# First norm of a hybrid layer: four of sixteen token tiles transposed by TensorE instead of by DMA

## The chip, the cores and the metric

The kernel runs on one core of a Trainium2 chip. The metric is the device time of one execution in microseconds. Engines are named as in the profile: PE is TensorE, DVE VectorE, ACT ScalarE, POOL GpSimd; SP is SyncE, which issues most DMAs.

## The reference

One layer, on x of 2048 tokens by 1024 columns in float32:

```
h = RMSNorm(x, g_mix);  z = h @ w_in          # columns: conv u | gate B | gate C | q | k | v
yA = B * causal_dwconv3(C * u)
yB = three dilated sliding-window attentions over 8 heads, mixed by their softmax sums
x = x + concat(RMSNorm(yA), RMSNorm(yB)) @ w_out
x = x + SwiGLU(RMSNorm(x))                    # 2816 hidden columns
```

The change sits in the first line: the norm of x, and the transposed form of h that the matmuls of w_in need.

## The kernel before, in words

Every large product is done in float16 with each factor split in a high part and a remainder ("hi" and "lo"); `mm3_steps` issues three matmuls for each 128 rows of the contraction (L187 to L189: high x high, high x low, low x high).

**The first norm.** The 2048 tokens are 16 tiles of 128 (`norm`, L248). For each tile the 128x1024 float32 block is loaded by SP (`nx_x`, for tiles 6 and 7 `qT`; L257), ACT squares it and sums the squares (L258), a short chain on ACT and DVE makes the reciprocal root (`rnorm`, L65 to L70), ACT writes the high part (L262) and DVE the remainder (L263) into a float16 tile `ka` or `kb`. Two DMA transposes, one for the high part and one for the remainder, then write them into `self.x[c][q]` (`b` in the profile), with the model's columns on the partitions; c is the chunk of 512 tokens, q is 0 for high and 1 for remainder. The profile shows these DMAs at L195. There are two buffers each of `ka` and `kb`, which the convolution also uses, so a later batch of tiles waits until the transposes of an earlier one have been read out.

**The matmuls around it.** `in_and_conv` first does tiles 0 to 3 (two calls of `norm`) with the weights of the first column group between them: `first(2)`, `first(0)`, `first(1)` load 128 columns each (`wraw`, L131), find their largest value on DVE (`vmax`, L92 on) and write them as high part (ACT, L145) and remainder (DVE, L146) into `wq`. Then `conv_steps` goes through four chunks c of 512 tokens. In each it does three groups of 24 matmuls (C, u and B, in this order) into PSUM tiles `cvx`, `cvx` and `mm`. The very first group is done in two halves of 256 tokens, so that it needs tiles 0 and 1 alone at first. Ahead of chunk c the function `before(c)` asks for the norm of the four tiles of chunk c+1. This is column group j=0; for j=1 and j=2 the chunks are gone through again with weights that are loaded and split meanwhile. The loads for j=1 are ordered behind the last transposes of the norm:

```python
with tc.issue_after(self.dve.ins), tc.issue_after(self.sp.ins):
    u1 = self.weights(cols(j + 1), ux, dst=(t1[:, 0], t1[:, 1]))[2]
```

Attention, the output projection and the SwiGLU follow; PE is busy nearly throughout.

**What sets the order.** Each engine works through its own queue in order. The order in the queues isn't written out: the framework's planner lays it out from the dependences and its own estimate of times (`schedule_with_timeline_sim=True`), earlier lines of the program going first where several are ready. `issue_after` adds single edges. SP's queue is in order too: a load behind a transpose waits until it has been issued.

PSUM has 8 banks here: 3 of `psmm` (tile `mm`), 4 of `cvx`, 1 of `pstr`.

Of the kernel before, what the change touches and what calls it, by code (L numbers as in the profile page):

```python
# [8 lines left out]
F32 = mybir.dt.float32  # L9
F16 = mybir.dt.float16  # L10
# [7 lines left out]
P = 128  # L18
S = 2048
D = 1024  # L20
KC = D // P
# [8 lines left out]
class Builder:  # L30
# [203 lines left out]
    def setup(self):  # L234

        nc, A, cp = self.nc, self.A, self.cp
        self.g_in = self.gains(cp, [A["g_mix"][0]], "gin", 0)
        make_identity(nc, self.ident32)
        nc.vector.memset(self.ones, 1.0)
        for i, b in enumerate(self.SHIFTS):  # L240
            nc.vector.memset(self.eps[:, i:i + 1], 4.0 ** -b * EPS)
        nc.scalar.square(self.ones, self.ones)
        self.yamax = cp.tile([P, 16], F32, name="yamax")
        self.ssa = cp.tile([P, NT], F32, name="ssa")
        self.uq = cp.tile([P, 5], F32, name="uq")
        self.uo = cp.tile([P, 2], F32, name="uo")
        self.wc = cp.tile([P, 4, 3], F32, name="convw")
        for t in range(3):  # L248
            nc.scalar.dma_start(self.wc[:, :, t], A["conv_w"][0, t].rearrange("(c p) -> p c", p=P))

    def norm(self, i, xt, hl):

        nc = self.nc
        n = len(xt)
        ss = self.nxs.tile([P, n], F32, name=f"nx_ss{n}")
        for j in range(n):
            nc.sync.dma_start(xt[j], self.A["x"][0][(i + j) * P:(i + j + 1) * P])  # L257
            nc.scalar.activation(hl[j][:, 0], xt[j], AF.Square, accum_out=ss[:, j:j + 1])  # L258
        r = self.rnorm(self.nxs, ss, n, D, f"nx{n}", 9)
        for j in range(n):  # L260
            h, l = hl[j][:, 0], hl[j][:, 1]
            nc.scalar.activation(h, xt[j], AF.Copy, scale=r[:, j:j + 1])  # L262
            self.dve = nc.vector.scalar_tensor_tensor(l, xt[j], r[:, j:j + 1], h, op0=ALU.mult, op1=ALU.subtract)  # L263
            c, t = (i + j) // 4, slice((i + j) % 4 * P, ((i + j) % 4 + 1) * P)
            for q in range(2):
                self.sp = self.transpose(self.x[c][q][:, :, t], hl[j][:, q])

# [95 lines left out]
    def in_and_conv(self):  # L363
        tc, nc, A = self.tc, self.nc, self.A
        w_in, w_out = A["w_in"][0], A["w_out"][0]
        with ExitStack() as c:
# [36 lines left out]
            for j in range(3):  # L403
                def before(c):
                    if j == 0 and c == 0:
                        norm(0, 2)
                        first(2)
                        norm(2, 2)
                        first(0)
                        with tc.issue_after(self.dve.ins):  # L410
                            first(1)
                    if j == 0 and c < 3:
                        if c == 2:
                            norm(4 * c + 4, 2)
                            norm(4 * c + 6, 2)
                        else:
                            norm(4 * c + 4, 4)
# [786 lines left out]
```

## Time and profile before

| | us |
|---|---|
| median of 3 runs | 2199.42 (2199.12 to 2206.35) |
| the profiled execution | 2203.85 |
| its span, first to last instruction | 2202.1 |
| PE busy in it | 2075.1 (94%) |
| DVE busy | 1458.2 (66%) |
| ACT busy | 1028.2 (47%) |
| POOL busy | 627.1 (28%) |

Times in the profile are microseconds from the start of the span. PE's busy time counts pipelined matmuls, so a busy PE is not one at its peak. A row of a timeline gives start, duration, engine, line, operation, out<-in with shapes, and how many were merged; brackets give the idle time before it and what ended it. SPq is the DMA queue of SP, and the duration of an issue there is the time that SP spent on it, not the time to landing.

### The profile page before, as it was taken

The page shows a single profiled execution, that of the slowest core. Times are in us where ns is not written, and L with a number is a line of the kernel's source. Part 1 is how long each engine was busy: PE and PEld are TensorE (multiplying, and loading weights), DVE is VectorE, ACT ScalarE, POOL GpSimd, SP SyncE. Part 2 cuts the span into 40 slices and gives each one's busy share as a digit, 9 for nine tenths or more (in the row PEclk, how much of TensorE's full clock was granted, in tenths as well). Part 3 has the DMA queues.
Part 4 walks back from the last instruction along what each step waited for, and adds up shares of the span by engine and source line. Part 5 has one row for each costly group of instructions (what it writes and reads, how often), then busy time and mean ns, then how long its engine had stood idle before and what let it go on. Part 6 is the DMA issues. An engine that isn't in the chain of part 4 may idle for free. (4 is left out here: it accounts for less than half of the span.)

```text
span 2202.1 us, 32820 instructions
## 1 busy us (share of the span) xinstructions
PE 2075.1 (94%) x11864; PEld 1080.4 (49%) x11864; DVE 1458.2 (66%) x3380; ACT 1028.2 (47%) x2134; POOL 627.1 (28%) x515
## 2 busy tenths in 40 slices
PE   4999999989889889979999999999999989999999
PEld 2344567767666644434444444444444434444444
DVE  5687447778876676785767676766676565545454
ACT  6443347676766655653333343333333243434341
POOL 0000133344343212212112111211121145555463
PEclk9999999999999989989999999999999999999999
DMA  9767458999989987899332233223322754251342
GB/s 244 168 201 245 110 121 150 197 180 184 178 163 211 213 206 220 246 280 244 101 105 87 96 110 100 92 87 110 101 91 91 242 195 140 59 191 53 116 142 96
DMA packets 555492, 339.64 MB, mean 154 GB/s; under 512 B 354624, under 2 KB 508224, under 8 KB 552896
## 3 DMA queue, kind: packets, MB, share of 16 engines
q1 hardware_dynamic: 537648, 314.38, 55.4%
q10 hardware_dynamic: 17680, 23.16, 3.0%
q8 instruction: 93, 1.52, 0.3%
q14 instruction: 71, 0.58, 0.1%
HBM read 161.24 MB, written 107.54 MB: 122 GB/s over the span
## 5 line engine op out<-in xcount | busy, mean ns | idle before, releaser
L1001 PEld LDWEIGHTS <-w 128*128 128x128 f16 x3696 | 362.6, 98 | 457.3 <-issue 18.4
L1001 PE MATMUL ps<-b,w 128*128 128x512 f16 x2112 | 465.4, 381 | 10.9 <-ACT s L1050 3.5
L1126 PE MATMUL ps<-b,w 128*128 128x512 f16 x1848 | 402.3, 381 | 6.2 <-ACT s L1137 5.3
L1001 PE MATMUL ps<-hb,w 128*128 128x512 f16 x1584 | 348.9, 380 | 4.9 <-DVE w_m L77 2.6
L1126 PEld LDWEIGHTS <-w 128*128 128x128 f16 x1848 | 181.4, 98 | 226.8 <-issue 10.6
L894 POOL TENSOR_TENSOR t<-wq 128x512 f32<-128x512 f32 (+1 forms) x46 | 60.4, 1312 | 442.5 <-issue 266.9
L187 PE MATMUL mm<-wq,b 128*128 128x384 f16 x512 | 170.9, 334 | 7.4 <-DVE vs L471 7.4
L1007 DVE TENSOR_TENSOR s<-ps,s 128x512 f32<-128x512 f32 x220 | 150.2, 683 | 36.4 <-PE ps L1001 35.8
L188 PE MATMUL mm<-wq,b 128*128 128x384 f16 x512 | 170.5, 333 | 0.0
L189 PE MATMUL mm<-wq,b 128*128 128x384 f16 x512 | 170.2, 332 | 0.0
L1133 POOL TENSOR_TENSOR x<-x,s 128x512 f32<-128x512 f32 x72 | 103.5, 1438 | 188.6 <-DVE s L1144 140.7
L1134 DVE SCALAR_TENSOR_TENSOR x<-ps,a_u,x 128x512 f32<-128x512 f32 x96 | 71.9, 750 | 109.3 <-PE ps L1126 80.7
L615 ACT ACTIVATE s<-s,u 128x256 f32<-128x256 f32 (+1 forms) x224 | 98.0, 452 | 66.5 <-DVE u L610 44.9
L911 ACT CAST w<-t 128x512 f16<-128x512 f32 x88 | 54.1, 617 | 142.0 <-PE ps L1001 75.6
L187 PEld LDWEIGHTS <-b 128*128 128x128 f16 x768 | 84.4, 110 | 70.7 <-ACT b L773 8.2
L610 DVE CUSTOM_DVE_ANT_0 s<-s,mask,nkap 128x256 f32<-128x256 f32 (+1 forms) x224 | 104.5, 482 | 20.0 <-PE s L605 14.4
L188 PEld LDWEIGHTS <-b 128*128 128x128 f16 x768 | 84.6, 110 | 65.2 <-issue 16.7
L189 PEld LDWEIGHTS <-b 128*128 128x128 f16 x768 | 84.2, 110 | 57.2 <-issue 5.4
L187 PE MATMUL cvx<-b,wq 128*128 128x512 f16 (+1 forms) x200 | 77.4, 390 | 31.3 <-ACT kb L262 25.0
L633 PE MATMUL av<-v,et 128*128 128x65 f16 x1800 | 78.5, 196 | 28.6 <-DMA et<-eh 19.0
L604 PE MATMUL s<-ka,qT 128*128 128x128 f16 (+1 forms) x408 | 91.1, 270 | 7.6 <-DVE eh L626 6.6
L1113 ACT CAST w<-t 128x512 f16<-128x512 f32 (+1 forms) x96 | 53.6, 581 | 90.6 <-PE ps L1126 75.3
(297 smaller groups left out, 3802.6 us busy)
## 6 DMA issues: line engine op xcount, KB each, us to landing
d_a<-a ACTq DMA_DIRECT2D x88, 256.0 KB, 2.0
d_wd<-w SPq DMA_DIRECT2D x77, 256.0 KB, 2.0
wq<-d_a SPq DMA_DIRECT2D x64, 256.0 KB, 4.1
b<-d_wd SPq DMA_DIRECT2D x14, 1024.0 KB, 7.7
wraw<-in_w_in_dram SPq DMA_DIRECT2D x24, 512.0 KB, 7.3
d_h<-hl SPq DMA_DIRECT2D x24, 512.0 KB, 3.0
wq<-in_w_gate_dram SPq DMA_DIRECT2D x22, 512.0 KB, 5.3
wq<-in_w_up_dram SPq DMA_DIRECT2D x22, 512.0 KB, 5.3
```

The costliest lines, as they stand in the source:

```text
L187: self.pe = mm(ps, lhsT=lh(k), rhs=rh(k), start=k == ks[0], stop=False)
L188: mm(ps, lhsT=lh(k), rhs=rl(k), start=False, stop=False)
L189: mm(ps, lhsT=ll(k), rhs=rh(k), start=False, stop=k == ks[-1])
L604: nc.tensor.matmul(o, lhsT=query(u), rhs=hi[x], start=True, stop=False)
L610: nc.vector.tensor_tensor_reduce(sm[:, at[u]], sp[:, at[u]], mask[:, P - P * has_prev(u):256], accum_out=Ub[:, u, HD + 1:HD + 2], op0=ALU.add,
L615: nc.scalar.activation(sm[:, at[u]], sm[:, at[u]], AF.Exp, scale=-1.0, bias=Ub[:, u, HD + 1:HD + 2])
L633: self.pe_av = nc.tensor.matmul(av[:, u - u0], lhsT=p_, rhs=v_, start=n_ == 0, stop=n_ == len(ops) - 1)
L1001: nc.tensor.matmul(ps[self.BANK[n]], lhsT=w[:, x, k], rhs=b[:, y, k], start=first and k == 0 and q == 0, stop=k == 3 and q == 2, skip_grou ...
L1007: nc.vector.tensor_tensor(t, x, y, op=ALU.add)
L1126: nc.tensor.matmul(ps[self.BANK[n]], lhsT=L[n][:, x, f], rhs=B[n][:, f, y], start=first and f == 0 and q == 0, stop=f == n_f - 1 and q == ...
L1133: nc.gpsimd.tensor_tensor(o, o, s_, op=ALU.add)
L1134: nc.vector.scalar_tensor_tensor(o, bank, u, o, op0=ALU.mult, op1=ALU.add)
```

## The change

A float16 copy of the identity is made at setup. In `norm`, the tiles of chunk 0 (0 to 3) are no longer transposed by DMA. For each of the high part and the remainder, eight matmuls take a 128x128 block as the stationary operand and the identity as the moving one, four into one bank of `psmm`; the bank is then copied as float16 into `self.x`, by ACT for the high part and by DVE for the remainder. Tiles 4 to 15 are transposed by DMA as before. That makes 64 matmuls, 8 copies on ACT and 8 on DVE in place of 8 DMA transposes.

```diff
--- before.py
+++ after.py
@@ setup
         nc.scalar.square(self.ones, self.ones)
+        self.ident16 = cp.tile([P, P], F16, name="ident16")
+        nc.vector.tensor_copy(self.ident16, self.ident32)
@@ norm
             c, t = (i + j) // 4, slice((i + j) % 4 * P, ((i + j) % 4 + 1) * P)
+            if c < 1:
+
+                for q in range(2):
+                    for k in range(0, KC, 4):
+                        ps = self.psmm.tile([P, 4, P], F32, name="mm")
+                        for m in range(4):
+                            self.pe = nc.tensor.matmul(ps[:, m], lhsT=hl[j][:, q, (k + m) * P:(k + m + 1) * P],
+                                                       rhs=self.ident16, start=True, stop=True)
+                        (nc.vector.tensor_copy if q else nc.scalar.copy)(self.x[c][q][:, k:k + 4, t], ps)
+                continue
             for q in range(2):
                 self.sp = self.transpose(self.x[c][q][:, :, t], hl[j][:, q])
```

## Rows read from the trace of the kernel before

**Rows 1.** Busy time by stretches: stretch, length, each engine, PEclk, DMA share, GB/s.

```profile
0.00:27.00 27.00, 0.37 (x1) 0.10 (x1) 16.38 (x66) 19.68 (x37) 0.70 (x6) 1.00 1.04 255
...
260.00:2202.00 1942.00, 1855.99 (x10839) 974.45 (x10837) 1280.58 (x2968) 914.93 (x1920) 612.39 (x482) 0.98 0.57 148
```

**Rows 2.** Waits of PE: who waited for whom: total, times, longest us.

```profile
PE cvx L187 <- ACT kb L262: 25.0, 1, 25.0
...
PE cvx L187 <- ACT wq L145: 3.8, 1, 3.8
```

**Rows 3.** Timeline of PE, 27 to 104 us.

```profile
27.45 0.40 PE L188 MATMUL cvx<-b,wq 128*128 128x256 f16 x1 [2.06 <-DMA b<-ka]
27.64 0.42 PE L189 MATMUL cvx<-b,wq 128*128 128x256 f16 x1
27.85 0.42 PE L187 MATMUL cvx<-b,wq 128*128 128x256 f16 x1
...
35.85 0.40 PE L188 MATMUL cvx<-b,wq 128*128 128x256 f16 x1 [1.54 <-DMA b<-kb]
...
51.06 0.59 PE L187 MATMUL cvx<-b,wq 128*128 128x512 f16 x2
...
103.47 0.61 PE L187 MATMUL cvx<-b,wq 128*128 128x512 f16 x1 [3.76 <-ACT wq L145]
```

**Rows 4.** Timeline of SP, the DMA queue, 15 to 90 us.

```profile
15.18 10.38 SPq L195 DMA_TRANSPOSE b<-ka  x4
...
26.76 7.20 SPq L195 DMA_TRANSPOSE b<-kb  x4
34.02 1.05 SPq L257 DMA_DIRECT2D nx_x<-in_x_dram  x2
35.17 7.26 SPq L195 DMA_TRANSPOSE b<-ka  x4
42.52 6.14 SPq L195 DMA_TRANSPOSE b<-kb  x4
...
55.55 5.38 SPq L195 DMA_TRANSPOSE b<-ka  x4
...
77.23 5.43 SPq L195 DMA_TRANSPOSE b<-kb  x4
82.71 7.79 SPq L131 DMA_DIRECT2D wraw<-in_w_in_dram  x6
```

**Rows 5.** Groups by line and form: out<-in xcount, busy us, mean ns, idle.

```profile
L1007 DVE TENSOR_TENSOR s<-ps,s 128x512 f32<-128x512 f32 x220 | 150.2, 683 | 36.4 <-PE ps L1001 35.8
...
L621 ACT CAST et<-pt 128x512 f16<-128x512 f32 x40 | 24.1, 602 | 6.1 <-PE pt L620 5.8
```

**Rows 6.** Timeline of DVE, 5 to 40 us.

```profile
5.65 0.16 DVE L92 TENSOR_REDUCE vm_a<-gin_g 128x1 f32<-128x8 f32 x1 [4.70 <-DMA gin_g<-in_g_mix_dram]
...
15.12 1.22 DVE L92 TENSOR_REDUCE vm_a<-wraw 128x1 f32<-128x1024 f32 x1 [0.68 <-DMA wraw<-in_w_in_dram]
...
24.00 2.48 DVE L263 SCALAR_TENSOR_TENSOR kb<-nx_x,nx_y,kb 128x1024 f16<-128x1024 f32 x2 [1.85 <-ACT kb L262]
...
32.11 2.48 DVE L263 SCALAR_TENSOR_TENSOR ka<-nx_x,nx_y,ka 128x1024 f16<-128x1024 f32 x2
...
36.90 2.18 DVE L146 SCALAR_TENSOR_TENSOR wq<-wraw,w_sg,wq 128x128 f16<-128x128 f32 x8
```

**Rows 7.** Timeline of ACT, 21 to 33 us.

```profile
21.77 1.06 ACT L258 ACTIVATE kb<-qT 128x1024 f16<-128x1024 f32 x1 [0.85 <-DMA qT<-in_x_dram]
...
30.93 2.19 ACT L262 ACTIVATE ka<-nx_x,nx_y 128x1024 f16<-128x1024 f32 x2 [2.36 <-DVE nx_y L70]
```

**Rows 8.** Busy time by stretches of 2 us, as in rows 1.

```profile
36.00:38.00 2.00, 2.00 (x11) 1.40 (x10) 2.00 (x6) 1.53 (x6) 0.00 (x0) 0.50 0.91 295
...
44.00:46.00 2.00, 2.00 (x11) 0.92 (x10) 0.00 (x0) 1.36 (x3) 0.00 (x0) 1.00 1.07 199
52.00:54.00 2.00, 2.00 (x11) 0.91 (x10) 1.24 (x6) 1.54 (x4) 0.00 (x0) 1.00 0.95 380
```

## The prediction

> **What bounds the kernel now.** I read the busy time by stretches first. From 260 us to the end TensorE (PE) is busy for 1856 of 1942 us; in the first 27 us it does next to nothing (0.37 us) [rows 1]. So the bulk is matmul time that this edit does not touch, and what it can change is how early the first stage lets PE run on. Next I read what PE waits for: 25.0 us before its first matmul is the longest wait of the whole execution, and the other long one in the front is 3.8 us for weights [rows 2].
>
> The timeline of PE places them. After a lone first matmul the stream proper begins at 27.45, released by the DMA transposes of token tiles 0 and 1. It stops again until those of tiles 2 and 3 have landed, at 35.85. From there it runs to 51.06, where chunk c=1 begins without a stall, and the 3.8 us of weights end at 103.47 [rows 3].
>
> The timeline of the DMA queue shows the other chain. SP issues the transposes of tiles 0 to 3 from 15.18 to 25.56 and from 26.76 to 33.96, four each; those of tiles 4 to 7 follow from 35.17 to 48.66 [rows 4]. PE reaches c=1 some 2.4 us behind the last of those issues. **So c=1 starts where two chains meet, with no slack in either**: PE's work on c=0, and the SP queue's transposes for c=1. An edit that shortens one alone gives nothing. From c=1 on the second chain goes on: each batch of tiles is written into buffers that the transposes before it must have left, and the raw weights of the next column group are loaded right behind the last transposes (77.23 to 82.66, load at 82.71) [rows 4].
>
> **The change, part by part.**
>
> *Removed:* 8 DMA transposes, 10.38 + 7.20 = 17.58 us of SP's queue [rows 4]. Uncontended ones go at 5.38 us for four (from 55.55), 1.35 us each [rows 4]; these were slower because x loads shared the engines.
>
> *Added:* 64 matmuls of 128 columns, 16 copies out of PSUM (8 on ScalarE, ACT, and 8 on VectorE, DVE), and one conversion of the identity. PE spaced its 256-column matmuls by 0.21 us there (27.64 to 27.85, [rows 3]), so 128 columns are at most that and, by width, 0.107: 64 x 0.107 = 6.8 us (13.6 at the upper end). Nearly all of it falls in time in which PE stands idle and costs nothing; the eight matmuls of the last half tile, 0.9 us, lie on the path. An ACT copy of just this form (128x512, float32 in PSUM to float16) takes 602 ns [rows 5]; 8 make 4.8 us. DVE has no such row. Its two-input 128x512 sum out of PSUM takes 683 ns [rows 5], which bounds a one-input copy from above; below stands ACT's 602, and 0.6 to 0.7 us it is. I take 0.65, the middle of two near ends; 8 make 5.2 us. The identity costs nothing: DVE stands idle for 4.70 us before its first reduction at 5.65 [rows 6].
>
> *What the copies delay.* On DVE two idle times of note lie between the first normalized tiles and tiles 4 to 7, 0.68 and 1.85 us [rows 6], together 2.5; the rest is work. So 5.2 us of copies push the float16 remainders of tiles 4 to 7 (32.11 to 36.9, [rows 6]) by 5.2 - 2.5 = 2.7 us. ACT has 2.36 us of idleness just before the same tiles [rows 7] and follows DVE there; I charge it nothing of its own. The ends are 0 (the copies fit into the holes) and 5.2 (no hole is used).
>
> *PE's chain.* The remainder of tile 3 ends at 26.48 today (24.00 + 2.48, [rows 6]), and the half chunk that needs it gets under way only at 35.85 [rows 3]: 9.4 us for issue, queue and landing. In the changed kernel the copies of tiles 0 and 1 push that remainder by at most 2.6 us, less the holes: 27.6. Behind it come 0.9 us of matmuls, two copies of 0.65 and their handovers, so the half chunk starts near 30.5 instead of 35.85. The first matmuls of c=0 can start as early as 20 instead of 27.45. Chunk c=0 ends 5.3 us earlier, 45.8 instead of 51.06. The weights of its third group, written by DVE from 36.90 to 39.1 [rows 6], shift to 42 and are needed at 40.7: its first matmuls may be held for an instant. The second half of c=0's first group ran at a granted clock of 0.50, the lower level [rows 8]; were it at full clock, PE would save 2.5 us more, and only wait longer for c=1.
>
> *SP's chain, which ends last.* Today the transposes for c=1 begin at 35.17, behind those of tiles 2 and 3 and two x loads [rows 4], although tile 4 was written by ACT from 30.93 on, at 1.09 us a tile [rows 7]. With the queue free they start when tile 4 is there: 32.0 + 2.7 = 34.7. Nothing else is in the engines by then (the loads of tiles 8 to 11 have gone before), so eight go in 8 x 1.35 = 10.8 us: the last issue ends at 45.5 instead of 48.66, 3.2 us earlier. The last remainder, 36.9 + 2.7 = 39.6, does not hold that. PE arrives at 45.8 and waits until about 47.9. I round the gain to 3.0 us. Every later batch waits for transposes before it, and the 3.8 us wait for weights hangs behind the last of these; so all of it shifts by the same 3 us, and beyond 260 us PE is full.
>
> [...] From 44 to 46 us, with transposes alone in the engines, 199 GB/s moved; from 52 to 54, with x loads alone, 380 [rows 8]. [...] The measurement says half the speed, so I stay with 1.35 us each.
>
> *The sum.* Profiled execution: 2203.85 us, span 2202.06. 2203.85 - 3.0 = 2200.85. The median of the runs shown is 2199.42, 4.4 below that execution; on its scale 2199.42 - 3.0 = **2196.4 us**.
>
> **The rivals.**
> *A, the forecast:* 3 us less, 2196.4, between 2193 and 2199. Chance 0.38.
> *B, the whole lead of PE passes through:* 7.5 us (27.45 - 20) at most by c=0's start, if tiles 4 to 7 are prepared earlier as well, since with an empty queue their x arrives sooner (ACT waits for it for 0.85 us at 21.77, [rows 7]). For it: the DMA engines are full through the first 27 us (share 1.04, [rows 1]). Against: ACT and DVE, not the loads, are what precedes tiles 4 to 7. Time 2199.42 - 7.5 = 2191.9; if the 3.8 us wait for weights closes too, 2188.1. Chance 0.22.
> *C, the copies are the new bound (slower):* all 16 land ahead of tiles 4 to 7 on DVE and ACT without using a hole, and the loads of tiles 10 and 11 still share the engines with the transposes, which then take today's 7.26 + 6.14 [rows 4]. Start 32.0 + 5.2 = 37.2, end 50.6 instead of 48.66: 1.9 us late, and 5.2 if the delay meets every later batch again: 2201.3 to 2204.6. It decides from a start later than 37.8 with fast transposes, or 35.2 with slow ones. Chance 0.18. [...] No row of the kernel before shows these copies in this stage.
> *D, swallowed later:* c=1 comes early, but the weights of the next group do not, because what precedes them (the load at 82.71, then DVE and ACT) does not move; the 3.76 us wait at 103.47 grows by the gain. Against it: that load follows the last transposes in SP's order. 2199.4, chance 0.12.
> *E, a new order elsewhere:* the planner lays out all engines' queues by its own simulated times, and the edit shifts these. Later stages may come out in another order, either way by 10 us or more. Nothing in the profile measures it. Chance 0.10.
>
> **How the numbers follow.** A, D, C and most of B lie between 2187 and 2204; outside remain B's far corner (0.05), part of C (0.03) and most of E (0.09). 0.5% of this time is 11 us, about what a measurement here can tell from no change (the three runs span 7 us). Faster than 2188.4: 0.06 from B's corner and 0.06 from E, 0.12. Slower than 2210.4: 0.04 from E, 0.03 from C if its delay returns with each batch, 0.07. The rest, 0.81, is no change by that measure, though A expects a small gain.
>
> **What would show it.** Right: eight transposes fewer in the queue; ACT and DVE copies of about 0.6 us between 13 and 31; PE's stream beginning near 20 to 22; the transposes of tiles 4 to 7 starting near 34.7 and ending near 45.5; a short wait of PE for them before c=1, near 48; c=2 and the wait for weights each about 3 us earlier. Wrong: c=1 starting at 51 or later (C), at 44 or earlier (B), a longer wait for weights (D), or stretches after 260 us that change by more than the front did (E).

## The result: 0.36% slower, though chunk c=1 came earlier, as forecast

| | median us (lowest to highest) | ratio to before, 95% interval |
|---|---|---|
| before, same chip | 2201.97 (2197.94 to 2209.53) | |
| changed | 2209.24 (2202.10 to 2219.29) | 1.0036 [1.0019, 1.0052] |

The medians are 7.3 us apart (7.9 by the ratio) where 3 us faster was forecast, and 2209.24 lies outside the forecast's 2193 to 2199. The profiled execution of the changed kernel took 2205.49 us with a span of 2203.7.

The profile after shows a front that came out near the forecast. First busy time by stretches; columns as in [rows 1].

```profile
0.00:27.00 27.00, 8.53 (x68) 6.82 (x69) 17.95 (x71) 21.52 (x41) 0.80 (x7) 1.00 0.88 254
260.00:2202.00 1942.00, 1854.61 (x10820) 972.87 (x10818) 1275.12 (x2955) 913.67 (x1919) 611.58 (x482) 0.98 0.57 148
36.00:38.00 2.00, 2.00 (x16) 1.43 (x15) 2.00 (x5) 2.00 (x3) 0.00 (x0) 1.00 0.83 154
44.00:46.00 2.00, 1.52 (x8) 0.48 (x5) 0.38 (x1) 1.61 (x4) 0.00 (x0) 1.00 1.03 188
```

PE works 8.53 us in the first 27 instead of 0.37 [rows 1]. The stretch from 36 to 38 us, at a granted clock of 0.50 before [rows 8], is now at 1.00. Next the waits of PE in the front, as in [rows 2], and its timeline, as in [rows 3].

```profile
PE mm L273 <- DVE w_sg L143: 13.0, 1, 13.0
...
PE cvx L187 <- ACT wq L145: 4.8, 1, 4.8
```

```profile
13.00 1.03 PE L273 MATMUL mm<-ident,ka 128*128 128x128 f16 x8 [13.00 <-DVE w_sg L143]
...
22.76 0.37 PE L188 MATMUL cvx<-b,wq 128*128 128x256 f16 x1 [0.55 <-DVE b L275]
...
30.81 0.49 PE L187 MATMUL cvx<-b,wq 128*128 128x256 f16 x2
...
32.71 0.27 PE L188 MATMUL cvx<-b,wq 128*128 128x256 f16 x1 [1.19 <-DVE b L275]
...
46.76 0.60 PE L187 MATMUL cvx<-b,wq 128*128 128x512 f16 x2 [1.24 <-DMA b<-kb]
...
48.10 0.38 PE L188 MATMUL cvx<-b,wq 128*128 128x512 f16 x1 [0.52 <-DMA b<-kb]
...
101.52 0.61 PE L187 MATMUL cvx<-b,wq 128*128 128x512 f16 x1 [4.80 <-ACT wq L145]
```

Two of the same matmuls in the kernel before, which [rows 3] leaves out:

```profile
33.81 0.50 PE L187 MATMUL cvx<-b,wq 128*128 128x256 f16 x2 [2.03 <-DMA b<-kb]
...
51.71 0.38 PE L188 MATMUL cvx<-b,wq 128*128 128x512 f16 x1
```

The reader is to see three things. The half chunk of tiles 2 and 3 starts at 30.81 instead of 33.81, and its first matmul that reads the remainder comes at 32.71 instead of 35.85. c=1 starts at 46.76 instead of 51.06, after a short wait for the transposes of tiles 4 to 7, the chain that was forecast to end last, and waits for them once more, until 48.10 (51.71 before). The wait for weights ends at 101.52 instead of 103.47, 1.95 us earlier. SP's queue, as in [rows 4], and the copies on DVE and ACT, as in [rows 6] and [rows 7]:

```profile
15.02 12.82 SPq L259 DMA_DIRECT2D nx_x<-in_x_dram  x4
35.08 5.50 SPq L195 DMA_TRANSPOSE b<-ka  x4
40.67 5.45 SPq L195 DMA_TRANSPOSE b<-kb  x4
...
79.49 8.04 SPq L131 DMA_DIRECT2D wraw<-in_w_in_dram  x6
```

```profile
17.36 0.68 DVE L275 CAST b<-mm 128x512 f16<-128x512 f32 x1
...
35.09 1.28 DVE L265 SCALAR_TENSOR_TENSOR ka<-nx_x,nx_y,ka 128x1024 f16<-128x1024 f32 x1
```

```profile
17.27 1.04 ACT L275 CAST b<-mm 128x512 f16<-128x512 f32 x2
```

Where did the lead go? The table sets each matmul of a trace against the same matmul in the kernel before and gives the median lateness in us, by the time of the kernel before (mean of its trace and that of run e1 below, which differ by up to 5.5 us ahead of 1000, 3.5 around 1000 and 8.7 at the end). The other columns are runs told below; e14 is the changed kernel itself on another chip. Each column is one execution.

| at us | changed | e14: changed, again | e5: before, half a block | e6: changed, whole block |
|---|---|---|---|---|
| 240 to 300 | -3.2 | 1.4 | 1.0 | 0.2 |
| 360 to 420 | -3.3 | 0.8 | 1.8 | 0.0 |
| 480 to 540 | -0.7 | 9.1 | 7.8 | 2.9 |
| 660 to 720 | 3.1 | 11.1 | 8.2 | 1.4 |
| 780 to 840 | 5.9 | 11.1 | 9.9 | 1.8 |
| 1020 to 1080 | 8.1 | 13.5 | 13.7 | -0.6 |
| from 2160 | 6.0 | 11.0 | 11.2 | -4.0 |

In the first column the changed kernel holds its 3 us until 420 and gives 11 back between 420 and 1020, in attention and what follows. In e14 the lead of the front is gone before that, for its wait for weights ends later:

```profile
103.79 0.61 PE L187 MATMUL cvx<-b,wq 128*128 128x512 f16 x1 [4.69 <-ACT wq L145]
```

The loss in attention is there again, 12.7 us up to 1020 to 1080. Between 420 and 1020 the queues of all engines stand in the same order as before, but for 780 to 835 us and one swap near 1005.

### The profile page after: what moved, and what is told of

It reads as the page before. It is cut to its first block, busy times and chain, and to the rows that moved or that the text cites. A ratio compares the mean times of both kernels' runs of the same rounds, so it can differ in the third digit from the quotient of the medians.

```text
span 2203.7 us, 32949 instructions
## 1 busy us (share of the span) xinstructions
PE 2079.5 (94%) x11928; PEld 1084.5 (49%) x11928; DVE 1460.1 (66%) x3389; ACT 1030.8 (47%) x2142; POOL 626.3 (28%) x515
## 3 DMA queue, kind: packets, MB, share of 16 engines
q1 hardware_dynamic: 529200, 312.28, 54.9%
## 5 line engine op out<-in xcount | busy, mean ns | idle before, releaser
L638 DVE TENSOR_TENSOR eh<-s,eh 128x512 f16<-128x512 f32 (+1 forms) x112 | 75.5, 677 | 30.9 <-ACT eh L637 30.5
```

Source lines behind the costliest of these rows:

```text
L638: nc.vector.tensor_tensor(eh[:, w:2 * w], sm[:, 0:w], eh[:, 0:w], op=ALU.subtract)
```

## The experiments

**First, the three differences that the change leaves behind.** Theory L: everything in SBUF lies 256 bytes further. Theory B: the banks of `mm` are taken in another rotation. Theory O: the other order of the queues at 780 to 835 us. Each run stands beside the kernel before on one chip; four runs share each chip.

*e1*: the identity alone.

```diff
+        self.ident16 = cp.tile([P, P], F16, name="ident16")
+        nc.vector.tensor_copy(self.ident16, self.ident32)
```

> The kernel before plus the float16 identity alone (one tile of 256 bytes a partition and one copy); all 16 tiles still go by DMA. Order of every queue as before; all later SBUF tiles lie 256 bytes higher, as in the changed kernel. Theory O (the 7 us come from the other order of the queues at 780 to 835 us and at 1005 us): like before, ratio 1.000 (2202 us). Theory L (they come from the shifted SBUF addresses): like the changed kernel, 1.003 to 1.004. Theory B (from the rotated PSUM banks of tile mm): 1.000, the banks are as before here.

Measured 0.9994 [0.9978, 1.0011]. L falls; the identity costs nothing.

*e2*: TensorE for tiles 2 and 3 alone.

```diff
-            if c < 1:
+            if 2 <= i + j < 4:
```

> The change for tiles 2 and 3 alone; tiles 0 and 1 go by DMA as before. From about 40 us on every queue stands in the order of the kernel before; SBUF is shifted by 256 bytes and mm's banks are rotated. The front should gain 2 to 4 us at c=1, since the transposes of tiles 4 to 7 still follow four transposes fewer. Theory O: 2199 us, ratio 0.998 to 0.999. Theory L: 1.003. Theory B: 1.003.

Measured 1.0016 [1.0000, 1.0032]. Its trace shows c=1 4.7 us early (46.36), and most of that gone by 450 us, with the queues in the order of before (but for one swap on ACT near 1738 us). So O can't be the whole of it.

*e3*: the changed kernel with the identity in another pool, so that SBUF lies as before.

```diff
-        self.ident16 = cp.tile([P, P], F16, name="ident16")
+        self.ident16 = self.rp.tile([P, P], F16, name="ident16")
```

> The changed kernel with the identity in a pool that is given back after the first stage, so that all later SBUF addresses are those of the kernel before; order of all queues as in the changed kernel, mm's banks rotated as there. Theory O: as the changed kernel, 1.003 to 1.004 (2209 us). Theory L: the front's gain alone, 0.998 to 0.999. Theory B: 1.003 to 1.004.

Measured 1.0039 [1.0024, 1.0054]. L falls again.

*e4*: the transposes go through the `cvx` banks, and those of `mm` rotate as before.

```diff
-                        ps = self.psmm.tile([P, 4, P], F32, name="mm")
+                        ps = self.cvx.tile([P, 4, P], F32, name="cvx")
```

> The changed kernel with the transposed blocks in the four banks of cvx in place of the three of mm: 16 uses of 4 banks leave every later bank of mm and cvx up to 780 us as in the kernel before. The queues' order at 780 to 835 us is a third one, neither before's nor after's. Front gain about 3 us as in the changed kernel. Theory B: 0.998 to 0.999. Theory L: 1.003 to 1.004. Theory O: by its own order, anywhere from 0.997 to 1.005, and then the difference must lie in the stretch from 780 to 1010 us.

Measured 1.0031 [1.0018, 1.0045]. B falls.

**A new theory from the traces.** In the kernels with TensorE transposes the stalls of PE in attention had other lengths, and attention's DMA transposes took another time to land, though nothing near them had changed. The page of the profile lists a DMA queue of instruction code, one like it in every kernel here; this is the changed kernel's:

```profile
PE 2079.5 (94%) x11928; PEld 1084.5 (49%) x11928; DVE 1460.1 (66%) x3389; ACT 1030.8 (47%) x2142; POOL 626.3 (28%) x515
...
q8 instruction: 93, 1.52, 0.3%
```

93 packets of 16 KB stand against 2 x 11,928 = 23,856 instructions of PE, one per 257; the trace shows each where PE has issued some 256 more (202 to 304, median 256). So q8 is taken to load PE's code, block by block (theory F). 64 added matmuls are 128 instructions with their weight loads: every later load comes half a block earlier in the work. The page counts the time of these loads (q8, 0.3%) and that of attention's transposes (in q1, 54.9%) on the same 16 DMA engines. Against F stands theory W: whatever the front wins is lost at a wait for something that doesn't come earlier.

The tool for it is a number of matmuls of one column, on the identity, that nobody reads. Put at the start of PE's queue they take 1.87 us for 64, while PE has nothing to do, and no queue changes its order beyond 40 us:

```profile
1.62 1.87 PE L267 MATMUL tr<-ident 128*128 128x1 f16 x64 [1.62 <-DVE ident L244]
```

*e5*: e1 plus 64 of them (half a block, as the change makes).

```diff
+            if i + j == 0:
+                ps = self.pstr.tile([P, 4], F32, name="tr")
+                for m in range(64):
+                    nc.tensor.matmul(ps[:, 0:1], lhsT=self.ident16, rhs=self.ident16[:, 0:1], start=True, stop=True)
```

> The kernel before (with the identity copy) plus 64 matmuls of one column on the identity, which nobody reads, ahead of everything else on PE, while it has nothing to do; all DMA transposes stay, and the queues of all engines keep the order of the kernel before. PE's code is loaded from memory in blocks of 16 KB, one per some 256 PE instructions in the traces so far; the 64 matmuls (128 instructions with their weight loads) shift every later load by half a block against the work, as the change itself does. Theory F (the loads of PE's code share the DMA engines with attention's transposes, and where they fall decides which transposes are late): slower by 4 to 10 us, ratio 1.002 to 1.0045, since the shift is there and no gain in front; the DMA waits of attention look like those of the changed kernel. Theory O (the other order of the queues at 780 to 835 us) and theory W (whatever is won in front is lost because attention waits for something that doesn't come earlier): no change, 0.999 to 1.001.

Measured 1.0057 [1.0040, 1.0074], 2207.64 against 2195.54: 12 us slower, without one change to a transpose. O and W say nothing of this; F does, though it had put it at 1.0045 at most.

*e6*: the changed kernel plus 64 (a whole block).

```diff
+                        for m in range(64 * (i + j + q + k == 0)):
+                            nc.tensor.matmul(ps[:, 0, 0:1], lhsT=self.ident16, rhs=self.ident16[:, 0:1], start=True, stop=True)
```

> The changed kernel plus the same 64 matmuls of one column: 256 PE instructions more than the kernel before, one whole block, so that the loads of PE's code fall back to the places in the work at which they were before. Order of all queues as in the changed kernel. Theory F: the loss of attention goes and the gain of about 3 us shows: 0.998 to 0.9995. Theory O and theory W: as the changed kernel, 1.003 to 1.004.

Measured 0.9999 [0.9987, 1.0010]: more work, and the loss is gone. The 3 us that F promised besides are not there.

The stall near 380 us shows how transposes land with and without a load in their flight. The rows are PE's timeline at the same matmul: in the kernel before, in e6, in the changed kernel and in e5.

```profile
381.95 0.54 PE L633 MATMUL av<-v,et 128*128 128x65 f16 x12 [1.31 <-DMA et<-eh]
```

```profile
382.03 0.54 PE L647 MATMUL av<-v,et 128*128 128x65 f16 x12 [1.26 <-DMA et<-eh]
```

```profile
379.10 0.54 PE L645 MATMUL av<-v,et 128*128 128x65 f16 x12 [2.71 <-DMA et<-eh]
```

```profile
384.75 0.82 PE L639 MATMUL av<-v,et 128*128 128x65 f16 x12 [2.56 <-DMA et<-eh]
```

The wait is 1.3 us with the loads in the old place and 2.6 to 2.7 us half a block off, whichever of the two kernels it is. The DMA queues in the 5 us ahead of it, packets and MB of PE's code, then issues and their time to landing in us, in the kernel before and in the changed kernel:

```profile
ka<-qkhl SPq DMA_TRANSPOSE x1, 3.3
kb<-qkhl SPq DMA_TRANSPOSE x1, 3.4
et<-eh SPq DMA_TRANSPOSE x1, 3.1
```

```profile
q8 instruction: 1, 0.02, 1.2%
ka<-qkhl SPq DMA_TRANSPOSE x1, 5.1
kb<-qkhl SPq DMA_TRANSPOSE x1, 4.6
et<-eh SPq DMA_TRANSPOSE x1, 3.8
```

In the kernel before no block is loaded in this stretch, in the changed kernel one is, and the three transposes land 1.8, 1.2 and 0.7 us later (e6: 3.3, 3.3, 3.1 without a load; e5: 4.9, 4.4, 3.8 with one). The packet's 1.2% of 16 engines over 5 us is 0.96 us of one engine's time, of the same size as the delays; that a transpose waits for that engine is not shown. Over all traces told here, transposes issued between 240 and 780 us land after 3.26 us (median of 1455) where no block of PE's code is loaded in their flight, and after 4.50 (638) where one is (those that meet a packet of q14, the page's other queue of instruction code, left out); for one and the same transpose, with a load in some traces and without in others, the difference is 1.0 us (median of 124). A long flight meets a load more easily than a short one, which makes the difference look larger; with only the loads within 2 us of the issue counted, 0.85 us are left (median of 105). A second cost follows. Busy time by 2 us right behind the stall, in the kernel before, in the changed kernel and in e5:

```profile
382.40:384.40 2.00, 2.00 (x17) 1.50 (x15) 1.44 (x3) 1.97 (x6) 0.06 (x1) 1.00 0.00 0
```

```profile
379.60:381.60 2.00, 2.00 (x10) 1.06 (x7) 1.60 (x5) 1.65 (x5) 1.21 (x1) 0.50 0.27 55
```

```profile
384.70:386.70 2.00, 1.95 (x18) 1.43 (x19) 1.38 (x2) 1.86 (x6) 0.49 (x1) 0.53 0.00 0
```

After the short stall the granted clock is 1.00, after the long ones 0.50 and 0.53, and in the changed kernel PE has 10 matmuls in the 2 us instead of 17: a stall that is 1.4 us longer has cost 3.0 us by 390 us. The number of transposes that meet a load hardly differs (53 in the kernel before, 46 in the changed one, 49 in e5); which ones do differs.

The cost of this stall doesn't last. The changed kernel is 4.3 us ahead of the kernel before when it comes to it, 1.2 ahead at 390 us and 3.2 ahead again at 400, where the kernel before has waits of its own; and the runs at three quarters of a block (e7, e10 and e12, told below), which are not slow, lose 2.6 to 2.9 us here and regain most of it. A stall that lasts is near 681 us. PE's rows there, in the kernel before and in the changed kernel:

```profile
680.97 0.54 PE L633 MATMUL av<-v,et 128*128 128x65 f16 x12
681.83 0.54 PE L633 MATMUL av<-v,et 128*128 128x65 f16 x12 [0.32 <-DMA et<-eh]
...
693.28 0.84 PE L633 MATMUL av<-v,et 128*128 128x65 f16 x12 [1.59 <-DMA et<-eh]
```

```profile
682.10 0.54 PE L645 MATMUL av<-v,et 128*128 128x65 f16 x12 [1.91 <-DMA et<-eh]
683.84 0.84 PE L645 MATMUL av<-v,et 128*128 128x65 f16 x12 [1.20 <-DMA et<-eh]
```

In all seven traces half a block off (the changed kernel, e3, e4, e5, e13, e14, e15) a block of PE's code is loaded in the flight of the two transposes that these waits are for; they land after 6.1 to 7.2 and 5.7 to 7.6 us. In the other eleven none is; they land after 5.0 to 5.9 and 4.5 to 5.5. (A packet of q14 falls there too, in all seven and in seven of the eleven.) Both waits together are 1.8 to 3.6 us in the seven and 0.4 to 2.1 in the others, and from 680 to 700 us the seven lose 2.8 us (mean) against the five traces with the loads in the old place (the kernel before, e1, e6, e9, e11), though three of the five wait 1.6 to 2.0 us once more, at 693.28 in the kernel before, and none of the seven does.

Not all of the loss is seen this way. Between the same two matmuls near 240 and 1060 us those five take 816 to 820 us and the seven 825 to 831, 9.0 more on the mean: 5.4 of them idle time of PE and 3.6 busy time, for the same number of matmuls. In the kernel before and in e5, columns as in [rows 1]:

```profile
239.94:1059.99 820.05, 747.89 (x5752) 477.97 (x5751) 583.35 (x1788) 495.78 (x1187) 240.03 (x201) 0.96 0.86 194
```

```profile
241.11:1071.99 830.88, 753.23 (x5752) 480.15 (x5751) 580.41 (x1788) 495.03 (x1188) 239.77 (x201) 0.95 0.86 191
```

But PE's waits for these transposes by name are hardly longer in sum (18.3 us against 17.6, means). Most of the added idle time stands at waits for DVE (for `eh` 11.0 us against 8.3) and for other transposes (`b` from `b`, 6.4 against 4.4). How the delay gets there was not followed. A rival, that PE runs out of its own code, is not seen: in these twelve traces none of its idle times over 0.15 us in this stretch ended without another engine or a DMA.

*e7* and *e8*: the changed kernel plus 32 and plus 96 (three quarters; a block and a quarter), with e6's edit.

> The changed kernel plus 32 such matmuls: PE's code is shifted by 192 instructions, three quarters of a block. Order as in the changed kernel. Theory F: another place for every load, so another time, anywhere from 0.998 to 1.004, but the same waits do not grow as in the changed kernel. Theories O and W: 1.003 to 1.004.

> The changed kernel plus 96 such matmuls: shift of 320 instructions, a block and a quarter, the places of the run with tiles 2 and 3 alone. Order as in the changed kernel. Theory F: near that run's 1.0016, 0.9995 to 1.0025. Theories O and W: 1.003 to 1.004.

Measured 1.0001 [0.9983, 1.0019] and 1.0021 [1.0009, 1.0034]. The half block's loss is gone from e7, and e8 lies between; their intervals overlap. e8 stands near e2, which has the same place.

*e9* and *e10*: e5's edit with 128 and with 96, on the kernel before. Rival T: the added matmuls cost by their number.

> The kernel before (with the identity copy) plus 128 matmuls of one column at the start, twice as many as in the run with 64: 256 PE instructions, one whole block. Order of the queues as before. Theory F (the place of the loads of PE's code decides): as before, 0.9985 to 1.0015, although there are twice as many added matmuls. Rival T (the added matmuls themselves cost, by their number): 1.005 or more, as much as the 64 or twice that.

> The same with 96: 192 PE instructions, three quarters of a block. Theory F: a third place of the loads; the changed kernel lost nothing to attention up to 780 us there, so 0.998 to 1.003. Rival T: between the run with 64 and that with 128, 1.005 or more.

Measured 0.9994 [0.9981, 1.0008] and 1.0010 [0.9998, 1.0023]. T falls: 128 cost nothing, 64 cost 12 us. In e9's trace the wait near 380 us is 1.24 us again.

*e11* and *e12*: e2 plus 96 and plus 64 at the start, as tries at a kernel better than both.

> TensorE transposes tiles 2 and 3 alone (64 PE instructions), and 96 matmuls of one column stand at the start (192 more): one whole block. Order of the queues beyond 40 us as before. Theory F: attention as in the kernel before, and the 3 to 4 us of the front stay: 0.9975 to 0.9995. If the lead is used up by any wait on the way (theory W): 1.000.

> The same with 64 matmuls at the start: 192 PE instructions in all, three quarters of a block. Order as before. Theory F: the place of the loads at which the changed kernel kept its lead up to 780 us and lost it behind, where its queues stand in another order; with the order of before the lead stays: 0.997 to 0.9995. Theory W: 1.000.

Measured 0.9991 [0.9982, 1.0001] and 0.9996 [0.9985, 1.0007]. Neither is told apart from no gain, and e12 misses the gain that F had put on it.

*e13* to *e16*, on one chip: e5's edit with 192, the changed kernel again, e2 plus 32, and e5's edit with 32.

> The kernel before (with the identity copy) plus 192 matmuls of one column at the start: a block and a half, 384 PE instructions. Theory F (the place of the loads of PE's code, periodic in a block of 256): as slow as with 64, 1.004 to 1.0075, although 128 cost nothing. Rival: no period, something particular to the run with 64: 0.999 to 1.002.

> The changed kernel as it is, on the same chip as the kernel before with half a block of shift. Theory F with the gain of 3 us at an equal place: 1.003 to 1.0045, that is 0.001 to 0.003 under the run with 192. If the change's lead is lost by itself: equal to the run with 192.

> Tiles 2 and 3 alone by TensorE, and 32 matmuls of one column: half a block, with the queues beyond 40 us in the order of the kernel before. Theory F: 1.0025 to 1.005, the changed kernel's time without its other order at 780 to 835 us. Theory O (that order costs): clearly below the changed kernel. A rival that the loss belongs to the transposes of tiles 0 and 1: 1.000 to 1.002.

> The kernel before plus 32: a quarter of a block, the place at which the runs with gain in front gave 1.0016 and 1.0021. Theory F with a gain of 3 us at an equal place: 1.0025 to 1.004. Without it: 1.0015 to 1.002.

Measured 1.0051 [1.0033, 1.0069], 1.0039 [1.0024, 1.0055], 1.0032 [1.0020, 1.0043] and 1.0005 [0.9991, 1.0019]. A block and a half is as slow as a half (1.0051 and 1.0057), a whole block as fast as none (0.9994 both), so as far as tried the effect is periodic in blocks. e15 keeps the order of before and is slow all the same: O is not the cause. e16's median missed its expectation under either reading.

All ratios by the place of the loads:

| shift of PE's code, in blocks | transposes all by DMA | two tiles by TensorE | four tiles |
|---|---|---|---|
| 0 or 1 | 0.9994, 0.9994 | 0.9991 | 0.9999 |
| 1/4 | 1.0005 | 1.0016 | 1.0021 |
| 1/2 | 1.0057, 1.0051 | 1.0032 | 1.0036, 1.0039, 1.0039, 1.0031 |
| 3/4 | 1.0010 | 0.9996 | 1.0001 |

Down a column the place decides over 12 to 14 us for kernels without TensorE transposes and 7 to 9 for those with them. Along a row the change is worth -0.0026 to +0.0016, and most of these intervals overlap: a gain near 3 us is seen at a half (2207.98 against 2205.11 on one chip, 2.9 us, not apart by the intervals) and one of 2 to 3 at three quarters (not apart either), none at a quarter or a whole.

## Why the prediction was wrong

*What bounds the kernel, and the two chains:* right in the main. c=1 waits for the DMA transposes, as SP's chain ending last demanded; it starts 4.3 us earlier in the profiled executions, and behind its second wait it is 3.6 us ahead (48.10 against 51.71; 3.2 forecast by SP's chain). Two small misses offset each other there. The last issue ends 2.5 us earlier (46.12 against 48.66), not 3.2; but "no slack in either" was off by about 1 us, for the last of these transposes landed at 50.53 in the kernel before, and the matmul behind it came at 51.71.

*The terms of the front:* nearly right. The transposes for c=1 run from 35.08 to 46.12 (34.7 to 45.5 forecast), 1.37 us each, at 188 GB/s, as the prediction had taken them. In the kernel before 380 GB/s moved from 52 to 54 us [rows 8], without transposes, but not "with x loads alone": a store of 256 KB (`d_ya`, issued at 52.05) was in the engines too. Half the speed holds against loads and store together, and PE waits for these transposes. A DVE copy took 0.68 us (0.65), an ACT copy 0.58 (0.602; the merged row of two shows 1.04 because they overlap), and tile 4's remainder moved by 3.0 us, from 32.11 [rows 6] to 35.09 (2.7). The first matmuls of c=0 came at 22.76, not 20. The half chunk's 35.85, the first matmul that reads the remainder, became 32.71 where 30.5 was forecast: the copies stood in DVE's queue behind 3.5 us of work on the weights (from 27.40 to 31.30). PE came to c=1 at 45.5 (45.8 forecast) all the same, because it then went at a granted clock of 1.00 instead of 0.50 (36 to 38 us), 256-column matmuls 0.11 us apart instead of 0.21; the prediction had named this saving of 2.5 us and not counted it. That the two offset each other is luck. The raw weights load 3.2 us earlier (79.49 against 82.71, [rows 4]), but the wait for them grew by 1.0 us, so 1.95 us of lead are left at 101.52: a little of rival D. In e14, the same kernel, none is left there (103.79 against 103.47). In the seven traces with four tiles on TensorE this wait ends between 101.2 and 103.8 us, in the seven with all tiles by DMA between 103.5 and 105.6.

*The step that failed:* "so all of it shifts by the same 3 us, and beyond 260 us PE is full". It holds as far as 420 us in the changed kernel's trace, and in e14's only to c=1. Beyond that PE is busy but not free of stalls, and the lengths of these change with where the loads of PE's code fall (near 380 us 1.3 us in the old place, 2.6 to 2.7 us half a block off). The 64 matmuls were priced at 6.8 us of PE and found hidden, which was right; that they are 128 instructions in front of everything that follows had no term in the sum. e5 measures that term by itself: +12 us. With the forecast gain of 3 this gives +9, against +7.3 to +7.9 measured.

*The rivals:* C (the copies as a new bound) did not come. E had the right place, "stretches after 260 us that change by more than the front did", and the wrong mechanism: the planner's new order is there at 780 to 835 us, but kernels without it (e5, e13, e15) lose as much. By the prediction's own measure of 11 us either way the result is "no change", to which it gave 0.81. That is luck: the 0.81 came from gains and losses in the front, and no rival let a hidden addition on PE cost anything later.

*What stays open:* why the lead of 3 us is not in the totals at two of the four places; the wait for weights takes all of it in some executions. In e6 it can be seen to end at one wait; these are PE's rows there, in the kernel before and in e6:

```profile
195.60 1.87 PE L335 MATMUL tr<-ones,sq 128*128 128x1 f32 x8 [3.59 <-POOL sq L328]
```

```profile
195.66 1.87 PE L349 MATMUL tr<-ones,sq 128*128 128x1 f32 x8 [5.75 <-POOL sq L342]
```

PE arrives 2.1 us earlier and waits 2.2 us longer for POOL. In the changed kernel the same wait is 2.9 us, and the lead passes. What makes POOL late in e6 was not tried apart. That the place of the loads decides is shown by the runs. That it acts by delaying transposes is shown for single stalls by the landing times; how these add up to 9 us is not shown.

## What to carry to other kernels

Here 128 instructions added at the start of PE's queue moved the loads of PE's code by half a block against all later work, and an edit that was free where it stood (1.87 us of idle PE) cost 12 us of 2196 elsewhere (e5, 1.0057). Before a difference of this size is put down to an edit, pad the engine's stream with cheap instructions to a whole block (256 of PE's instructions here), or time it at several paddings, and compare at the same place. Whether a kernel whose DMA transposes have slack is less open to this was not tried.

## What the runs showed of the hardware that was not expected

PE's code came in packets of 16 KB, one for every 256 or so of its instructions (93 for 23,856), and a transpose with one such packet in its flight landed 1.0 us later (median). PE itself is not seen to wait for code: in twelve traces none of its idle times over 0.15 us between 240 and 1060 us ended without another engine or a DMA. But the kernel as a whole paid, for the same work with the loads half a block away took 12 us more (e5, 2207.64 against 2195.54). In the changed kernel TensorE also came to its faster pace earlier: its 256-column matmuls are 0.21 us apart until 24.4 us and 0.11 from 24.6 on (until 30.6 and from 30.8 before), and the stretch from 36 to 38 us was granted 1.00 where before it was 0.50 [rows 8]. That the transposes did this was not tried apart.
